# Conv input held in SBUF, three kinds of load on another queue, transposes for a broadcast, and one-operand steps on ScalarE, in a two-layer hybrid decoder trunk

## The chip, the cores and the metric

The kernel runs on one core of one Trainium2 chip. The metric is the device time of one execution in microseconds (us). Engines are named as the profile names them: PE is TensorE (PEld its weight loads), DVE is VectorE, ACT is ScalarE, POOL is GpSimd, SP is SyncE, which here only issues DMAs. POOL issues DMAs too, through a queue of its own.

## The reference, cut to what matters

Two layers over 1024 tokens of width 1024, all in float32. Each layer is

```
u = rmsnorm(h) @ W_in                       # split among three head groups
A = sparse attention: an indexer of 16 heads scores every causal key, the 256
    best keys per query are kept, softmax attention runs over them (8 heads)
B = conformer conv: y = a * sigmoid(g); causal depthwise conv of width 31;
    y = silu(layernorm(y + conv_b)); y @ conv_pw            # 256 channels
C = trailing means over 2/4/8/16 tokens minus the token, a small matmul, a scale
h += rmsnorm(concat(A, B, C) @ W_out)
h += rmsnorm(relu(rmsnorm(h) @ W_up)^2 @ W_down)
h += sigmoid(h @ W_gate) * (p @ W_ple)
```

## The kernel before, in words

Channels lie on the 128 lanes, tokens along the row; a row is half the sequence, 512 tokens ("hf" 0 or 1). Every large product is a *unit*: one 128-wide block of output channels, 24 matmuls of 128x512 (three per block of 128 input channels, since operands are split into a high and a low part; `dense`, L239). Weights come on SP's queue into two `wraw` buffers (`prepare`, L196), ACT writes the high part (L204), POOL the low part (L205). A unit's output lies in one of three PSUM buffers `pd`; five more, `bank`, serve everything else.

The order is written out in `PHASES`: a *win* phase (input projection, 21 units) and an *m* phase (output projection, MLP, gate: about 80 units) for each layer and half. Beside the units run the conv, the pooling and the attention of the halves whose projection is done, as generators in the list `bg`. `run` (L1074) gives them a share: each unit adds its cost times the phase's entry of `RATES` to a budget, each step of a generator spends some. This fixes the order of the program; a planner then fills each engine's queue by simulated times, preferring what is earlier in the program. At run time each engine, and each DMA queue, works its list strictly in order.

Buffers are rings (`Ring`, L98): `get` takes the one that was given back longest ago, and the planner adds a wait when its last user is on another engine. `dtmp` (11 rows of 512), `ctmp` (5), `row` (5 of 1088 columns) matter here.

- **Conv** (`conv_pool`, L455). In the win phase the gated input y is made in a `dtmp` (L385, L391) and stored to HBM (`cpS`, L392). `window` (L468) reads 30 + 512 columns of both channel blocks back into a `row`. Then 62 taps on DVE, each a 128x512 step into a bank (L535 for tap 0, L537 for the others). The layer norm takes a mean over the 256 channels: `token_sums` (L294: matmuls against a column of ones), a division on DVE (L551), and `spread` (L300: four matmuls against an identity that copy a value per token to all lanes). The tail (L565 to L571) ends in two more matmul groups.
- **rms** (L305): token sums, one small step on DVE, a power on POOL, `spread`. It runs in every norm: `rms_sb`, `post_norm`, and the conv.
- **Selection** (`select`, L655), the 256 best keys of each query: 31 rounds of bisection on 16-bit halves of the scores. A round counts for each of the blocks how many scores lie below a trial value. In the second half (hf 1) there are four blocks, of 640, 768, 896 and 1024 keys: ACT counts the two middle ones (L683), DVE the other two (L669), and each count writes flags that nobody reads into a scratch buffer of the ring `spare`, which in hf 1 is the ring `row`; two of its buffers are held by the 16-bit halves. Ahead of and behind the rounds stand row-wide multiplications (L713, L742) and the step that makes the mask (L755).
- **Attention** (`attend`, L815) uses `row` for the probabilities in hf 1: two for the step at hand, two for the one before.
- **Loads** on POOL's queue: keys (`kd`, L613), values (`vst`, L836), queries (`qst`, L608), and the eight inputs of the output projection (`slot<-mixS`, L923).

Of the kernel before, what the change touches and what calls it, by code (L numbers as in the profile page):

```python
# [8 lines left out]
F32 = mybir.dt.float32  # L9
# [6 lines left out]
AF = mybir.ActivationFunctionType  # L16
OP = mybir.AluOpType
# [16 lines left out]

RATES = (1.171, 1.114, 0.558, 0.766, 0.722, 0.567, 0.741, 0.946)

# [50 lines left out]
def tile_trunk(ctx: ExitStack, tc: tile.TileContext, xT, pT, pos, vecs, invf, cinv,  # L87
# [28 lines left out]
    vS = dram.tile([DEPTH, 2, P, 8, P], F32, name="vS")  # L116
    cpS = dram.tile([DEPTH, 512, S], F32, name="cpS")
    eS = dram.tile([DEPTH, NK, P, S], F32, name="eS")
# [6 lines left out]
    wlo = Ring("wlo", 4, [P, 4, P], F32R)  # L125
    dtmp = Ring("dtmp", 11, [P, HALF])
    ctmp = Ring("ctmp", 5, [P, HALF])
    cmat = Ring("cmat", 6, [P, HALF], F32R)
    rows = Ring("row", 5, [P, 1088])
    qst = Ring("qst", 2, [P, 4, P], F32R)  # L130
# [20 lines left out]
    sy.dma_start(cv, cinv)  # L151
    jp = const.tile([P, P], F32, name="jp")
    gp.iota(jp, pattern=[[1, P]], base=0, channel_multiplier=-1, allow_small_or_imprecise_dtypes=True)
    ident = const.tile([P, P], F32, name="ident")
    ve.tensor_scalar(ident, jp, 0.0, None, op0=OP.is_equal)
    ones = const.tile([P, 1], F32, name="ones")
    ve.memset(ones, 1.0)
    mhalf = const.tile([P, 4], F32, name="mhalf")
    ve.memset(mhalf, -0.5)
# [3 lines left out]
    ve.memset(cbias, 0.0)  # L163
    ve.tensor_scalar(cbias[:, P:], jp, 0.0, -BIG, op0=OP.is_gt, op1=OP.mult)
    wiT = const.tile([P, DEPTH, 8, 16], F32, name="wiT")
    rbs = Ring("rb", 1, [P, HALF])


    fr = const.tile([P, 2], F32, name="fr")
    halfpi = const.tile([P, 1], F32, name="halfpi")  # L170
    ve.memset(halfpi, math.pi / 2)
    sc.activation(halfpi, halfpi, AF.Copy)
# [127 lines left out]
    def spread(ps, t4):  # L300

        for j in range(4):
            te.matmul(ps[:, j * P:(j + 1) * P], t4[:, j:j + 1].to_broadcast([P, P]), ident, start=True, stop=True)

# [20 lines left out]
    def win_phase(l, hf, xs, sq):  # L325
# [12 lines left out]

        def evac(ps, lanes=slice(0, P), half=False):
            x = dtmp.get()  # L340
            if half:
                ve.scalar_tensor_tensor(x[lanes], ps[lanes], 0.5, rb[lanes], op0=OP.mult, op1=OP.mult)
            else:
                ve.tensor_tensor(x[lanes], ps[lanes], rb[lanes], op=OP.mult)
            return x
# [31 lines left out]
        held = None  # L377
        conv = {}
        for name in win_order(l, hf):
# [4 lines left out]
            if kind == "A":  # L384
                conv[name[1]] = evac(ps, half=True)  # L385
            elif kind == "G":
                c = int(name[1])
                g = scaled(ps)
                sc.activation(g, g, AF.Tanh, scale=0.5)
                y = conv[name[1]]  # L390
                ve.scalar_tensor_tensor(y, g, 1.0, y, op0=OP.add, op1=OP.mult)  # L391
                sy.dma_start(cpS[l, c * P:(c + 1) * P, ts], y)  # L392
                dtmp.put(y)
            elif kind == "P":
                c = int(name[1])
                x = evac(ps)
                sy.dma_start(cpS[l, 256 + c * P:256 + (c + 1) * P, ts], x)
                dtmp.put(x)
                if c == 1:
                    bg.append(((l, hf), conv_pool(l, hf)))  # L400
            elif name in ("M0", "I0"):
# [52 lines left out]

    def conv_pool(l, hf):  # L455
        t0 = hf * HALF
# [10 lines left out]

        def window(r0, n):  # L468

            t = rows.get()  # L470
            x = t[:, :2 * (n + HALF)].rearrange("p (c t) -> p c t", c=2)
            src = cpS[l, r0:r0 + 256].rearrange("(c p) t -> p c t", p=P)
            if hf == 0:
                gp.memset(x[:, :, :n], 0.0)
                sy.dma_start(x[:, :, n:], src[:, :, ts])
            else:
                sy.dma_start(x, src[:, :, t0 - n:t0 + HALF])
            return t, x
# [14 lines left out]
        wt, cw = small_weights(0, 2)  # L493
        pt_, pus = window(256, 15)
        for c in range(2):
# [29 lines left out]

        yt, yc = window(0, TAPS - 1)
        at = rows.get()
        acc = at[:, :1024].rearrange("p (c t) -> p c t", c=2)
        for c in range(2):
            pa = banks.get()  # L530
            for k in range(TAPS):
                w = vl[:, V_DW + c * TAPS + k:V_DW + c * TAPS + k + 1]
                src = yc[:, c, k:k + HALF]
                if k == 0:
                    ve.tensor_scalar(pa, src, w, vl[:, V_CONV_B + c:V_CONV_B + c + 1], op0=OP.mult, op1=OP.add)  # L535
                else:
# [4 lines left out]
        rows.put(yt)  # L541
        while (l, hf) == (0, 0) and ("index", l, hf) not in state:
# [4 lines left out]
        gp.tensor_tensor(both, acc[:, 0], acc[:, 1], op=OP.add)  # L547
        token_sums(ps, [both])
        ctmp.put(both)
        mu = tiny("mu")  # L550
        ve.tensor_scalar(mu, ps[:, :4], 1.0 / 256, None, op0=OP.mult)  # L551
        spread(ps, mu)
        sq = [ctmp.get(), ctmp.get()]
# [9 lines left out]
        for c in range(2):  # L563
            a = acc[:, c]
            ve.scalar_tensor_tensor(a, a, vl[:, V_LN_G + c:V_LN_G + c + 1], ps, op0=OP.mult, op1=OP.mult)  # L565
            th = ctmp.get()
            sc.activation(th, a, AF.Tanh, scale=0.5, bias=hb[:, l, c:c + 1])
            ve.tensor_scalar(a, a, vl[:, V_LN_B + c:V_LN_B + c + 1], 0.5, op0=OP.add, op1=OP.mult)
# [18 lines left out]
    def attention(l, hf):  # L587
# [23 lines left out]
        def load_k(h, k0, n):  # L611
            for dup in range(2):
                gp.dma_start(kd[dup * 64:(dup + 1) * 64, :, k0:k0 + n],  # L613
                             kS[l, :, :, :n].rearrange("k (d h) t -> h d k t", h=3)[h])
# [16 lines left out]
        def index():  # L631

            load_k(2, 0, Ws[-1])
            for j, b in enumerate(sel):
                W = Ws[j]
                for h in range(16):
                    if h % 4 == 0:
                        q = load_q(qiS, b, h, 16)
                    w = wiT[:, l, b, h:h + 1]
                    for n0, n1, ps in scores(q[:, h % 4], W, 0):  # L640
                        r, at = ps[:, :n1 - n0], idx[j][:, n0:n1]
                        sc.activation(r, r, AF.Relu)  # L642
                        if h == 0:
                            ve.tensor_scalar(at, r, w, None, op0=OP.mult)
                        else:
                            ve.scalar_tensor_tensor(at, r, w, at, op0=OP.mult, op1=OP.add)  # L646
                        banks.put(ps)
                    if h % 4 == 3:
                        qst.put(q)
                    yield W * 1.32 / 1024  # L650
                gp.affine_select(idx[j][:, W - P:], idx[j][:, W - P:], pattern=[[-1, P]], compare_op=OP.is_ge,
                                 fill=LOW, base=0, channel_multiplier=1)
            state["index", l, hf] = True

        def select():  # L655
# [56 lines left out]
            for j in range(nb):  # L712
                ve.tensor_scalar(idx[j], idx[j], sg[:, j:j + 1], None, op0=OP.mult)  # L713
                w0 = Ws[j - 1] if j % 2 else 0
                top.append(packed[j // 2].bitcast(I16)[:, w0:w0 + Ws[j]])
                ve.tensor_copy(top[j], idx[j].bitcast(I16)[:, 1::2])
# [24 lines left out]
            for j in range(nb):  # L741
                ve.tensor_scalar(idx[j], idx[j], sg[:, j:j + 1], None, op0=OP.mult)  # L742
            count(idx, thr, OP.is_gt, need)
# [3 lines left out]
            for j in range(nb):  # L747
# [6 lines left out]
                ve.scalar_tensor_tensor(idx[j], idx[j], thr[:, j:j + 1], e, op0=OP.is_gt, op1=OP.add)  # L754
                ve.tensor_scalar(idx[j], idx[j], -1.0, BIG, op0=OP.add, op1=OP.mult)  # L755
                spare.put(et, ct)
# [58 lines left out]
        def attend(some, at, ring):  # L815
# [3 lines left out]
            for step in [(kv, b, g) for kv in range(2) for b in some for g in (0, 2)] + [None]:  # L819
# [10 lines left out]
                if before:  # L830
                    (bkv, bb, bg), bpr = before
                    v0 = 4 * bkv if hf == 0 else 0
                    if bg == 0:
                        po = banks.get()
                        if bb == some[0]:
                            gp.dma_start(vst[:, v0:v0 + n // P], vS[l, bkv, :, :n // P])  # L836
                    yield from weighted(po, bb, (bg, bg + 1), v0, bpr, ring)
# [83 lines left out]
    def load(xs, ks, ts):  # L921
        for k in ks:
            gp.dma_start(xs[k], mixS[:, k * P:(k + 1) * P, ts].rearrange("k p t -> p k t"))  # L923

# [239 lines left out]
```

## Time and profile before

| | |
|---|---|
| time, median of 3 runs | 2843.78 us (2837.95 to 2844.03) |
| the profiled execution's own time | 2843.85 us |
| its span | 2842.1 us |
| PE busy / share of the chain that ended last | 2720.5 us / 72% |
| DVE busy / share of the chain | 1747.6 us / 16% |
| ACT busy / share of the chain | 1548.1 us / 3% |
| POOL busy / share of the chain | 1418.0 us / 1% |
| DMA, share of the chain | 5% |
| mean granted TensorE clock | 0.985 of 2.4 GHz |

The span runs from the first to the last instruction; the time of the execution holds 1.75 us more around it. Busy time of PE is the union of overlapping matmuls: one 128x512 matmul is on record for 0.39 us, but in a steady stretch a new one starts every 0.23 us. The chain goes back from the last instruction to whatever released each step, so its shares say what the end waited for, and the busy shares only what ran.

### The profile page before, as it was taken

The page shows a single profiled execution, that of the slowest core. Times are in us where ns is not written, and L with a number is a line of the kernel's source. Part 1 is how long each engine was busy: PE and PEld are TensorE (multiplying, and loading weights), DVE is VectorE, ACT ScalarE, POOL GpSimd, SP SyncE. Part 2 cuts the span into 40 slices and gives each one's busy share as a digit, 9 for nine tenths or more (in the row PEclk, how much of TensorE's full clock was granted, in tenths as well). Part 3 has the DMA queues.
Part 4 walks back from the last instruction along what each step waited for, and adds up shares of the span by engine and source line. Part 5 has one row for each costly group of instructions (what it writes and reads, how often), then busy time and mean ns, then how long its engine had stood idle before and what let it go on. Part 6 is the DMA issues. An engine that isn't in the chain of part 4 may idle for free.

```text
span 2842.1 us, 37724 instructions
## 1 busy us (share of the span) xinstructions
PE 2720.5 (96%) x12648; PEld 2242.8 (79%) x12648; DVE 1747.6 (61%) x3473; ACT 1548.1 (54%) x2932; POOL 1418.0 (50%) x1161
## 2 busy tenths in 40 slices
PE   7899989999999999899999989999999999999998
PEld 6677777887888878778788777888878878788886
DVE  7969679788447775965822467587985561511123
ACT  5347667775567535766334423677757654533343
POOL 4655425444334665544544755444443356544446
PEclk9999999999999999999999999999999999999999
DMA  5676554422343576533333547534223354423233
GB/s 189 198 192 218 153 134 148 112 85 90 93 115 106 159 238 187 162 116 102 114 104 104 184 152 238 152 116 108 97 79 98 104 164 138 155 97 99 98 97 122
DMA packets 195666, 384.90 MB, mean 135 GB/s; under 512 B 17424, under 2 KB 76944, under 8 KB 195472
## 3 DMA queue, kind: packets, MB, share of 16 engines
q1 hardware_dynamic: 138192, 330.58, 35.7%
q0 software_dynamic: 57280, 51.91, 8.7%
q8 instruction: 100, 1.64, 0.3%
q14 instruction: 94, 0.77, 0.1%
HBM read 307.97 MB, written 74.45 MB: 135 GB/s over the span
## 4 chain that ended last, share of the span: by engine, by line
PE 72%; DVE 16%; DMA 5%; ACT 3%; issue 3%; POOL 1%; SPq 0%; POOLq 0%; DVEq 0%; ACTq 0%
PE pd L243 20%; PE pd L249 20%; PE pd L248 20%; PE bank L601 5%; DVE bank L537 2%; PE bank L789 2%; DVE dtmp L875 1%; DVE row L669 1%; DVE slot L261 1%; DMA row<-cpS 1%; PE bank L798 1%; PE bank L797 1%; DVE cmat L261 1%; PE pd L298 1%; DVE dtmp L261 1%
## 5 line engine op out<-in xcount | busy, mean ns | idle before, releaser
L205 POOL TENSOR_TENSOR wlo<-wraw,whi 128x512 fp32r<-128x512 f32 x824 | 1094.7, 1334 | 1180.6 <-ACT whi L204 1115.4
L243 PE MATMUL pd<-slot,whi 128*128 128x512 f32 x3296 | 1306.8, 397 | 50.7 <-DVE slot L261 14.5
L248 PE MATMUL pd<-slot,whi 128*128 128x512 f32 x3168 | 1246.0, 393 | 4.6 <-DVE slot L261 2.7
L249 PE MATMUL pd<-slot,wlo 128*128 128x512 f32 x3168 | 1241.9, 393 | 4.1 <-POOL wlo L205 4.0
L204 ACT ACTIVATE whi<-wraw 128x512 fp32r<-128x512 f32 x824 | 511.1, 627 | 731.3 <-PE pd L248 499.0
L243 PEld LDWEIGHTS pd<-slot,whi 128*128 128x128 f32 x3296 | 625.6, 190 | 188.4 <-DVE slot L261 16.6
L249 PEld LDWEIGHTS pd<-slot,wlo 128*128 128x128 f32 x3168 | 600.0, 189 | 130.9 <-POOL wlo L205 7.5
L248 PEld LDWEIGHTS pd<-slot,whi 128*128 128x128 f32 x3168 | 601.1, 190 | 125.8 <-DVE slot L266 3.9
L601 PE MATMUL bank<-kd,qst 128*128 128x512 f32 (+3 forms) x1024 | 261.5, 360 | 10.6 <-DVE mxc L767 3.7
L646 DVE SCALAR_TENSOR_TENSOR idx<-bank,wiT,idx 128x512 f32<-128x512 f32 (+3 forms) x300 | 189.3, 652 | 94.7 <-ACT bank L642 90.7
L601 PEld LDWEIGHTS bank<-kd,qst 128*128 128x128 f32 x1024 | 181.7, 192 | 46.6 <-DVE idx L646 6.8
L642 ACT ACTIVATE bank<-bank 128x512 f32<-128x512 f32 (+2 forms) x320 | 153.8, 506 | 90.0 <-PE bank L601 85.2
L981 DVE SCALAR_TENSOR_TENSOR pd<-pd,rb 128x512 f32<-128x512 f32 x112 | 77.7, 694 | 183.2 <-PE pd L249 183.2
L995 DVE TENSOR_TENSOR yT<-yT,pd 128x512 f32<-128x512 f32 x96 | 65.5, 684 | 197.8 <-PE pd L249 197.5
L537 DVE SCALAR_TENSOR_TENSOR bank<-row,vec,bank 128x512 f32<-128x512 f32 x232 | 162.1, 746 | 0.5
L669 DVE TENSOR_SCALAR_CACHE_REDUCE row<-row,cc 128x640 f32<-128x640 uint16 (+1 forms) x124 | 133.5, 1077 | 14.5 <-ACT row L683 12.6
L683 ACT ACTIVATE row<-row,cc 128x768 f32<-128x768 uint16 (+1 forms) x124 | 121.5, 983 | 18.0 <-DVE cc L689 15.3
L767 DVE CUSTOM_DVE_ANT_0 row<-bank,idx 128x512 f32<-128x512 f32 (+3 forms) x160 | 91.4, 591 | 64.0 <-PE bank L601 60.6
L261 DVE TENSOR_TENSOR cmat<-bank,cmat 128x512 fp32r<-128x512 f32 (+1 forms) x160 | 97.9, 631 | 49.4 <-ACT cmat L260 43.8
L261 DVE TENSOR_TENSOR slot<-pd,slot 128x512 fp32r<-128x512 f32 x112 | 76.6, 685 | 51.3 <-ACT slot L260 51.1
L982 ACT ACTIVATE pd<-pd 128x512 f32<-128x512 f32 x112 | 65.2, 582 | 72.8 <-DVE pd L981 72.7
L775 ACT ACTIVATE row<-row,nmc 128x384 f32<-128x384 f32 (+5 forms) x96 | 84.2, 878 | 27.8 <-DVE nmc L771 21.0
(216 smaller groups left out, 2828.7 us busy)
## 6 DMA issues: line engine op xcount, KB each, us to landing
wraw<-wup SPq DMA_DIRECT2D x128, 512.0 KB, 3.3
wraw<-wdown SPq DMA_DIRECT2D x128, 512.0 KB, 3.3
wraw<-win SPq DMA_DIRECT2D x84, 512.0 KB, 4.2
qiS<-dtmp SPq DMA_DIRECT2D x64, 256.0 KB, 2.5
slot<-mixS POOLq DMA_DIRECT2D x32, 512.0 KB, 7.0
wraw<-wgate SPq DMA_DIRECT2D x32, 512.0 KB, 3.6
qst<-qiS POOLq DMA_DIRECT2D x48, 256.0 KB, 3.7
hS<-yT SPq DMA_DIRECT2D x48, 256.0 KB, 3.6
```

Source lines behind the costliest of these rows:

```text
L204: sc.activation(hi, r, AF.Copy)
L205: gp.tensor_tensor(lo, r, hi.bitcast(F32), op=OP.subtract)
L243: te.matmul(ps, wh, xh, start=i == 0, stop=False)
L248: te.matmul(ps, wh, xl, start=False, stop=False)
L249: te.matmul(ps, wl, xh, start=False, stop=i == n - 1)
L261: ve.tensor_tensor(lo, src, hi.bitcast(F32), op=OP.subtract)
L537: ve.scalar_tensor_tensor(acc[:, c] if k == TAPS - 1 else pa, src, w, pa, op0=OP.mult, op1=OP.add)
L601: te.matmul(ps[:, :n1 - n0], q, kd[:, k, k0 + n0:k0 + n1], start=k == 0, stop=k == 1)
L642: sc.activation(r, r, AF.Relu)
L646: ve.scalar_tensor_tensor(at, r, w, at, op0=OP.mult, op1=OP.add)
L669: ve.tensor_scalar(flags[:, :Ws[j]], of[j], t, None, op0=op, op1=OP.add, accum_out=dst[:, j:j + 1])
L683: sc.activation(flags[:, :Ws[j]], of[j], AF.Sign, scale=-1.0, bias=c[:, j:j + 1], accum_out=cnt[:, j:j + 1])
```

## The change

- `spread` uses TensorE's transpose in place of a matmul.
- The conv's input is written straight into one of two new buffers `win` (two channel blocks of 30 + 512 columns). The 30 columns in front are zeros in the first half; in the second they are a copy (ACT) of the last 30 of the first half, kept in `halo`. Only the pooling's input still goes through HBM (`plS`). Tap 0 moves to ACT.
- The conv's mean is one matmul of 128x512 against a 128x128 matrix of 1/256, which gives the mean on all lanes; token sums, division and spread go.
- On ACT in place of DVE: tap 0 (L535), the step L568, the index's first head (L644), and in the selection L713, L742 and L755.
- On SP's queue in place of POOL's: `kd`, `vst` and `slot<-mixS`. The queries stay.
- `dtmp` has 9 buffers (was 11), `row` 4 (was 5). Three of the eight `RATES` change.

```
-RATES = (1.171, 1.114, 0.558, 0.766, 0.722, 0.567, 0.741, 0.946)
+RATES = (1.205, 1.114, 0.558, 0.766, 0.751, 0.567, 0.731, 0.946)
-    dtmp = Ring("dtmp", 11, [P, HALF])
+    dtmp = Ring("dtmp", 9, [P, HALF])
-    rows = Ring("row", 5, [P, 1088])
+    rows = Ring("row", 4, [P, 1088])
+    wins = Ring("win", 2, [P, 2, TAPS - 1 + HALF])
+    halo = const.tile([P, 2, TAPS - 1], F32, name="halo")
...
-            te.matmul(ps[:, j * P:(j + 1) * P], t4[:, j:j + 1].to_broadcast([P, P]), ident, start=True, stop=True)
+            te.transpose(ps[:, j * P:(j + 1) * P], t4[:, j:j + 1].to_broadcast([P, P]), ident)
...
-                conv[name[1]] = evac(ps, half=True)
+                c = int(name[1])
+                if c == 0:
+                    yc = wins.get()
+                    if hf == 0:
+                        gp.memset(yc[:, :, :TAPS - 1], 0.0)
+                    else:
+                        sc.activation(yc[:, :, :TAPS - 1], halo, AF.Copy)
+                ve.scalar_tensor_tensor(yc[:, c, TAPS - 1:], ps, 0.5, rb, op0=OP.mult, op1=OP.mult)
...
-                y = conv[name[1]]
+                y = yc[:, c, TAPS - 1:]
                 ve.scalar_tensor_tensor(y, g, 1.0, y, op0=OP.add, op1=OP.mult)
-                sy.dma_start(cpS[l, c * P:(c + 1) * P, ts], y)
-                dtmp.put(y)
+                if c == 1 and hf == 0:
+                    sc.activation(halo, yc[:, :, HALF:], AF.Copy)
...
-        yt, yc = window(0, TAPS - 1)
...
-                    ve.tensor_scalar(pa, src, w, vl[:, V_CONV_B + c:V_CONV_B + c + 1], op0=OP.mult, op1=OP.add)
+                    sc.activation(pa, src, AF.Identity, scale=w, bias=vl[:, V_CONV_B + c:V_CONV_B + c + 1])
...
-        token_sums(ps, [both])
+        te.matmul(ps, mean256, both, start=True, stop=True)
         ctmp.put(both)
-        mu = tiny("mu")
-        ve.tensor_scalar(mu, ps[:, :4], 1.0 / 256, None, op0=OP.mult)
-        spread(ps, mu)
...
-                gp.dma_start(kd[dup * 64:(dup + 1) * 64, :, k0:k0 + n],
+                sy.dma_start(kd[dup * 64:(dup + 1) * 64, :, k0:k0 + n].bitcast(F32),
...
-                ve.tensor_scalar(idx[j], idx[j], sg[:, j:j + 1], None, op0=OP.mult)
+                sc.activation(idx[j], idx[j], AF.Copy, scale=sg[:, j:j + 1])
...
-                ve.tensor_scalar(idx[j], idx[j], -1.0, BIG, op0=OP.add, op1=OP.mult)
+                sc.activation(idx[j], idx[j], AF.Identity, scale=BIG, bias=nbig)
...
-            gp.dma_start(xs[k], mixS[:, k * P:(k + 1) * P, ts].rearrange("k p t -> p k t"))
+            sy.dma_start(xs[k].bitcast(F32), mixS[:, k * P:(k + 1) * P, ts].rearrange("k p t -> p k t"))
```

## Rows read from the trace of the kernel before

**Rows 1.** The page: busy time of each engine with its share of the span, and the chain that ended last by engine.

```profile
PE 2720.5 (96%) x12648; PEld 2242.8 (79%) x12648; DVE 1747.6 (61%) x3473; ACT 1548.1 (54%) x2932; POOL 1418.0 (50%) x1161
...
PE 72%; DVE 16%; DMA 5%; ACT 3%; issue 3%; POOL 1%; SPq 0%; POOLq 0%; DVEq 0%; ACTq 0%
```

**Rows 2.** Busy time by stretch: start and end, length, then busy us (instructions) of PE, PEld, DVE, ACT, POOL, the granted clock, the DMA share, GB/s. In order: units alone (a late MLP), the conv stages of (layer 0, half 0), (0, 1), (1, 0) and (1, 1), the rounds of the hf 1 selection of layer 0 and its tail, the rounds and the tail of layer 1, and the end of the win phase ahead of the m phase of (0, 1).

```profile
2450.00:2730.00 280.00, 280.00 (x1241) 232.02 (x1240) 54.67 (x78) 104.51 (x175) 135.45 (x105) 1.00 0.30 99
...
50.00:150.00 100.00, 82.15 (x331) 65.01 (x331) 87.93 (x121) 36.65 (x63) 56.00 (x45) 0.90 0.62 197
...
955.00:1055.00 100.00, 96.45 (x464) 79.36 (x463) 83.36 (x117) 33.79 (x60) 66.33 (x57) 1.00 0.67 199
1335.00:1400.00 65.00, 62.56 (x285) 50.83 (x284) 60.94 (x91) 21.24 (x37) 32.93 (x29) 1.00 0.42 128
1660.00:1750.00 90.00, 80.94 (x347) 65.31 (x345) 78.44 (x103) 27.02 (x47) 53.84 (x45) 0.96 0.62 193
...
606.00:659.00 53.00, 53.00 (x235) 43.92 (x234) 44.92 (x124) 42.51 (x84) 23.50 (x19) 1.00 0.30 98
660.00:695.00 35.00, 28.62 (x115) 22.51 (x113) 34.97 (x46) 11.65 (x22) 16.47 (x10) 0.90 0.22 69
2017.00:2075.00 58.00, 58.00 (x257) 48.04 (x257) 52.60 (x134) 45.13 (x88) 27.53 (x21) 1.00 0.29 97
2075.00:2112.00 37.00, 30.30 (x127) 24.34 (x126) 36.90 (x48) 12.52 (x23) 16.32 (x11) 0.95 0.22 74
...
1050.00:1088.00 38.00, 38.00 (x186) 32.19 (x185) 19.22 (x30) 18.06 (x36) 19.07 (x17) 1.00 0.71 218
```

**Rows 3.** Groups of PE instructions by line: the transposes of the attention, then token sums (L298) and spreads (L303) of the norms and of the conv; busy us and mean ns, then the idle time ahead of them.

```profile
L789 PE MATMUL bank<-ident,row 128*128 128x128 f32 x528 | 77.0, 276 | 1.4 <-DVE ctmp L807 1.4
...
L303 PE MATMUL pd<-ident,rrd 128*128 128x128 f32 x64 | 9.9, 297 | 5.0 <-POOL rrd L311 5.0
...
L303 PE MATMUL pd<-ident,rrn 128*128 128x128 f32 x64 | 8.7, 274 | 0.0
...
L298 PE MATMUL bank<-ones,ctmp 128*128 128x1 f32 x64 | 7.6, 239 | 0.0
L303 PE MATMUL bank<-ident,muc 128*128 128x128 f32 x32 | 4.2, 274 | 0.0
L303 PE MATMUL bank<-ident,rrc 128*128 128x128 f32 x32 | 4.2, 274 | 0.0
```

**Rows 4.** The conv's way through HBM: who waited for the DMAs of `cpS` (us, times), and the group of tap 0 (busy us, mean ns, idle ahead of it).

```profile
  DVE bank L535: 19.7, 4
  POOL row L499: 15.4, 4
...
L535 DVE TENSOR_SCALAR bank<-row,vec 128x512 f32<-128x512 f32 x8 | 6.3, 809 | 19.7 <-DMA row<-cpS 19.7
```

**Rows 5.** One-operand steps. First the DVE time of L713, L742 and L755 over the whole span, one line each in this order; then the spread of L755 (min/median/max ns); then ACT multiplying a row by a factor per lane (L777), widest and narrowest of six widths.

```profile
0.00:2842.10 2842.10, 8.88 (x12) 0.98 0.45 135
...
0.00:2842.10 2842.10, 9.20 (x12) 0.98 0.45 135
...
0.00:2842.10 2842.10, 12.12 (x12) 0.98 0.45 135
...
L755 DVE TENSOR_SCALAR idx<-idx x12: 517/828/1634, 304.1 to 2115.1; 128x384 f32<-128x384 f32 x2, 128x512 f32<-128x512 f32 x2, 128x640 f32<-128x640 f32 x2, 128x768 f32<-128x768 f32 x2
...
L777 ACT ACTIVATE row<-row,ric 128x1024 f32<-128x1024 f32 x16 | 18.2, 1144 | 0.7 <-DVE ric L776 0.7
...
L777 ACT ACTIVATE row<-row,ric 128x384 f32<-128x384 f32 x16 | 9.4, 607 | 0.7 <-DVE ric L776 0.7
```

**Rows 6.** One round of the selection of layer 1, hf 1, in order of time (start us, us, engine): first DVE, then ACT.

```profile
2029.15 0.88 DVE L669 TENSOR_SCALAR_CACHE_REDUCE row<-row,cc 128x640 f32<-128x640 uint16 x1
...
2030.27 1.28 DVE L669 TENSOR_SCALAR_CACHE_REDUCE row<-row,cc 128x1024 f32<-128x1024 uint16 x1 [0.16 <-ACT row L683]
...
2032.05 0.88 DVE L669 TENSOR_SCALAR_CACHE_REDUCE row<-row,cc 128x640 f32<-128x640 uint16 x1
...
2029.21 0.94 ACT L683 ACTIVATE row<-row,cc 128x768 f32<-128x768 uint16 x1 [0.20 <-DVE cc L689]
2030.05 0.19 ACT L683 ACTIVATION_READ_ACCUMULATOR row<-row,cc 128x1 f32 x1
...
2031.08 0.19 ACT L683 ACTIVATION_READ_ACCUMULATOR row<-row,cc 128x1 f32 x1
```

**Rows 7.** Loads: issue time on POOL (min/median/max ns) of the eight inputs; median landing times of POOL's and SP's loads of 512 KB; the longest waits of SP's queue and PE's wait for the inputs (us in total, times, longest).

```profile
L923 POOL DMA_DIRECT2D slot<-mixS x32: 696/733/805, 170.2 to 2334.2; - x32
...
wraw<-win SPq DMA_DIRECT2D x84, 512.0 KB, 4.2
slot<-mixS POOLq DMA_DIRECT2D x32, 512.0 KB, 7.0
...
SPq L199 <- POOL wlo L205: 1677.3, 377, 20.5
...
PE pd L243 <- DMA slot<-mixS: 5.0, 2, 2.8
```

**Rows 8.** The norm behind the MLP, last phase: POOL's five additions in a row, and the landing of the rows they add.

```profile
2789.05 8.07 POOL L876 TENSOR_TENSOR yT<-dtmp,dtmp 128x512 f32<-128x512 f32 x5 [1.89 <-DVE dtmp L875]
...
dtmp<-hS SPq DMA_DIRECT2D x48, 256.0 KB, 3.2
```

More of the change, by code (lines that the diff above doesn't have):

```diff
@@ L116, in tile_trunk @@
     vS = dram.tile([DEPTH, 2, P, 8, P], F32, name="vS")
-    cpS = dram.tile([DEPTH, 512, S], F32, name="cpS")
+    plS = dram.tile([DEPTH, 256, S], F32, name="plS")
     eS = dram.tile([DEPTH, NK, P, S], F32, name="eS")
@@ L151, in tile_trunk @@
     sy.dma_start(cv, cinv)
-    jp = const.tile([P, P], F32, name="jp")
+    lent = dtmp.get()
+    jp = lent[:, :P]
     gp.iota(jp, pattern=[[1, P]], base=0, channel_multiplier=-1, allow_small_or_imprecise_dtypes=True)
@@ L157, in tile_trunk @@
     ve.memset(ones, 1.0)
+    mean256 = const.tile([P, P], F32, name="mean256")
+    ve.memset(mean256, 1.0 / 256)
     mhalf = const.tile([P, 4], F32, name="mhalf")
@@ L164, in tile_trunk @@
     ve.tensor_scalar(cbias[:, P:], jp, 0.0, -BIG, op0=OP.is_gt, op1=OP.mult)
+    dtmp.put(lent)
     wiT = const.tile([P, DEPTH, 8, 16], F32, name="wiT")
@@ L170, in tile_trunk @@
     halfpi = const.tile([P, 1], F32, name="halfpi")
+    nbig = const.tile([P, 1], F32, name="nbig")
+    ve.memset(nbig, -BIG)
     ve.memset(halfpi, math.pi / 2)
@@ L337, in table, with evac @@
             return out
-        def evac(ps, lanes=slice(0, P), half=False):
+        def evac(ps, lanes=slice(0, P)):
             x = dtmp.get()
[L341 to L344, printed above, removed]
+            ve.tensor_tensor(x[lanes], ps[lanes], rb[lanes], op=OP.mult)
             return x
@@ L377, in win_phase @@
         held = None
-        conv = {}
         for name in win_order(l, hf):
@@ L396, in win_phase @@
                 x = evac(ps)
-                sy.dma_start(cpS[l, 256 + c * P:256 + (c + 1) * P, ts], x)
+                sy.dma_start(plS[l, c * P:(c + 1) * P, ts], x)
                 dtmp.put(x)
                 if c == 1:
-                    bg.append(((l, hf), conv_pool(l, hf)))
+                    bg.append(((l, hf), conv_pool(l, hf, yc)))
             elif name in ("M0", "I0"):
@@ L451, in win_phase, with conv_pool @@
         rbs.put(rb)
-    def conv_pool(l, hf):
+    def conv_pool(l, hf, yc):
         t0 = hf * HALF
@@ L466, in small_weights, with window @@
             return (hi, lo), [(hi[:, j * P:(j + 1) * P], lo[:, j * P:(j + 1) * P]) for j in range(n)]
-        def window(r0, n):
+        def window(n):
             t = rows.get()
             x = t[:, :2 * (n + HALF)].rearrange("p (c t) -> p c t", c=2)
-            src = cpS[l, r0:r0 + 256].rearrange("(c p) t -> p c t", p=P)
+            src = plS[l].rearrange("(c p) t -> p c t", p=P)
             if hf == 0:
@@ L493, in conv_pool @@
         wt, cw = small_weights(0, 2)
-        pt_, pus = window(256, 15)
+        pt_, pus = window(15)
         for c in range(2):
@@ L540, in conv_pool @@
             banks.put(pa)
-        rows.put(yt)
+        wins.put(yc)
         while (l, hf) == (0, 0) and ("index", l, hf) not in state:
@@ L567, in conv_pool @@
             sc.activation(th, a, AF.Tanh, scale=0.5, bias=hb[:, l, c:c + 1])
-            ve.tensor_scalar(a, a, vl[:, V_LN_B + c:V_LN_B + c + 1], 0.5, op0=OP.add, op1=OP.mult)
+            sc.activation(a, a, AF.Identity, scale=0.5, bias=hb[:, l, c:c + 1])
             ve.scalar_tensor_tensor(th, th, 1.0, a, op0=OP.add, op1=OP.mult)
@@ L643, in index @@
                         if h == 0:
-                            ve.tensor_scalar(at, r, w, None, op0=OP.mult)
+                            sc.activation(at, r, AF.Copy, scale=w)
                         else:
@@ L741, in select @@
             for j in range(nb):
-                ve.tensor_scalar(idx[j], idx[j], sg[:, j:j + 1], None, op0=OP.mult)
+                sc.activation(idx[j], idx[j], AF.Copy, scale=sg[:, j:j + 1])
             count(idx, thr, OP.is_gt, need)
@@ L835, in attend @@
                         if bb == some[0]:
-                            gp.dma_start(vst[:, v0:v0 + n // P], vS[l, bkv, :, :n // P])
+                            sy.dma_start(vst[:, v0:v0 + n // P].bitcast(F32), vS[l, bkv, :, :n // P])
                     yield from weighted(po, bb, (bg, bg + 1), v0, bpr, ring)
```

## The prediction

> **What bounds the kernel now.** I read the page first: PE is busy 96% of the span and carries 72% of the chain that ended last; DVE carries 16%, though it is busy only 61% [rows 1]. So mostly PE is the limit, and in some stretches DVE is. The view by stretch says which. A late MLP shows PE alone: 1241 matmuls in 280 us, 0.2256 us each, at full clock [rows 2]; a unit of 24 costs 5.4 us, and nothing but fewer or shorter PE instructions helps there. The four conv stages look different. In 50 to 150 DVE is busy 87.9 of 100 us, PE idles 17.85 and the granted clock falls to 0.90; the idle time of PE in the other three is 3.55, 2.44 and 9.06 us, 32.9 in all [rows 2]. Here a late DVE holds PE up. In the rounds of the selection PE has no idle time at all, but in the two tails behind them DVE is full (34.97 of 35, 36.90 of 37 us) and PE idles 6.38 and 6.70 us [rows 2]. The gains must come from these three places: PE's own work, conv stages, tails.
>
> **1. Spread by transposes, mean by one matmul.** A spread is recorded as 8 matmuls, two per block; the attention's transposes of the same 128x128 blocks have one record each, 77.0/528 = 0.146 us [rows 3]. The 160 records of the norms' spreads take 9.9 + 8.7 + 4.2 = 22.8 us; 80 transposes at 0.146 take 11.7: 11.1 us less. The mean loses its spread (4.2) and half of the conv's token sums (3.8), and gets one full-precision matmul of 512 columns in each of four stages; by columns that equals a spread, so 4.2 in all: 3.8 less. Sum 14.9 us. All of it is PE work, and a spread is also a link of its norm's chain, so nearly all counts; I take -14, with ends -16 and -7 (half of it idles instead).
>
> The terms of "TensorE: Matmul & The Clock Gate" in the Trainium skill call transpose mode four times faster for float32. By that the norms' spreads would fall to 5.7 us and this term to about -21. The attention's transposes here stand at half the records of the matmul form, not a quarter, so the sum goes by the row.
>
> **2. The conv input in SBUF.** DVE stood 19.7 us before tap 0, waiting for the four reads of `cpS`; tap 0 itself costs DVE 6.3 us [rows 4]. Both go, 26 us of DVE over four stages. Next late is the gated input itself, then ACT's tap 0, one 128x512 step on an engine that is busy 21 to 37 us of each such stage [rows 2]. What queues behind DVE's wait for it is tap 1 and, if ACT is late, the evacuation of PE's units. PE can win at most its 32.9 us of idle time, and only where DVE is full: about 7 us in the first stage, 4 in the last, none in the middle two, where PE idles under 4%. I take -11; ends -30 and 0. L568 on ACT frees DVE for eight short steps behind the taps: nothing. The pooling still comes through HBM, and its wait on POOL (15.4) stays [rows 4].
>
> **3. One-operand steps on ACT.** L713, L742 and L755 hold DVE 8.88 + 9.20 + 12.12 = 30.2 us; 36 ACT steps between 0.607 and 1.144, mean 0.876, take 31.5 [rows 5]. The selection's own chain thus stays as long, and DVE is freed of 30 us, of which only L755 stands in a tail: four steps, some 4 us in each hf 1 tail, of PE's 13.1 us of idle time there. The softmax then waits for ACT instead. I take -3; ends -10 and +5. The index's first head (L644) lies where neither engine is full: nothing.
>
> The rules of "ScalarE: Activation LUTs" in the Trainium skill speak against this: a plain multiplication or addition belongs on VectorE. A median step of L755 on DVE does take 0.828 us, but single ones reach 1.634 [rows 5]. By the medians the move loses a little time per step, by the measured sums nearly none, and the sum goes by these.
>
> **4. One `row` less.** This edit costs, and the diff does not show it. In hf 1 the selection's scratch comes from `row`: five less two packed ones is three, and now two. A round takes four: ACT, ACT, DVE, DVE. With three, only DVE's second count waits, for ACT's first; the row of the 1024 count says so: 0.16 us, released by L683. With two, DVE's first count waits for ACT's first (ends 2030.24) and its second for ACT's second (ends 2031.27). In the round shown DVE's second count starts at 2030.27; it would start at 2031.27: 1.0 us more on a round of 2.90 [rows 6]. That is 31 us in each of two selections, 62 in all. PE is full through the rounds [rows 2], and the evacuations of the units fit into the new gaps, so the time is only lost if the attention behind ends late: for half 1 of layer 0, ahead of the m phase at 1088, DVE has 38.0 - 19.2 = 18.8 us to spare [rows 2]. I take +6; ends 0 and +62. In the attention four buffers are just what two steps hold; PE is full there: nothing.
>
> **5. Loads on SP's queue.** Issuing one input takes POOL 0.733 us, and 512 KB land in 7.0 us; SP's weight loads of that size land in 4.2 [rows 7]. PE waited 5.0 us for the inputs, and POOL, which makes the weights' low parts, loses 76 issues. Against it: SP stands 1677 of 2842 us, 4.4 each time, waiting for a weight buffer [rows 7]; a load planned behind that waits too, and a load that waits for its data holds the next weight load. Two weight buffers cover 2 x 5.4 us of PE, more than a landing. I take -4; ends -9 and +18 (four m phases, each one such wait late).
>
> **6. Nine `dtmp` and the rest.** The conv no longer holds any. In the norm behind the MLP four rows of the embedding and two scratch rows leave three for the residual instead of five. POOL adds one row each 8.07/5 = 1.6 us; three buffers give 4.8 us for a landing of 3.2 [rows 8]. Covered, +1; if not, one landing in each of four norms, +13. The new `RATES` only move where steps stand in the program; no row prices that: 0, between -5 and +5 by PE's idle time in a tail.
>
> **Sum.** -14 - 11 - 3 + 6 - 4 + 1 + 0 = -25 against the profiled execution's own 2843.85, which stands within 0.1 us of the median: 2819 us.
>
> **Rivals.**
> - *The rounds arrive late* (slower). If the 62 us of part 4 reach the end in place of the 6, the time is 2819 - 6 + 62 = 2875. It decides from the point where more than 31 of the 62 come through, since the other terms give -31. For it: the rounds' DVE counts stand on the chain's DVE share, and the m phase needs that attention. Against: PE is full for the whole of the rounds, so that dense work is ready, and 18.8 us of slack lie ahead of the first deadline.
> - *SP's queue pushes back* (no change). Moved loads queue behind weight waits at all four starts: +18 for -4, 2841. For it: SP waits 59% of the span. Against: stores already go through that queue, and PE's waits for DMAs are small.
> - *Only PE's own work counts.* DVE's relief is eaten by what follows on DVE in the conv stages: terms 2 and 3 are nothing: 2833. For it: DVE stays full of taps. Against: the first conv stage has 17.85 us of idle PE.
> - *The conv stages recover in full*, -30 for -11, clock included: 2800.
>
> **Chances.** A measurement of this kernel tells about 0.2% (5.7 us) from no change. Forecast 0.48 (own range 2805 to 2835), late rounds 0.14, SP's queue 0.12, PE's work only 0.14, full recovery 0.12. Faster: 0.48 + 0.12 + 0.12 from the third = 0.72, less 0.02 for a forecast that ends at its upper edge: 0.70. Same: 0.08 from SP's queue and the 0.04 left over: 0.12. Slower: 0.14 and 0.04: 0.18. The range 2796 to 2854 takes in three of the four rivals and leaves out late rounds from about two thirds on.
>
> **What would show it.** Spreads with 4 records and half the time; no wait ahead of tap 1 over 1 us; less idle PE in the first and last conv stages and a clock back towards 1.00 there; rounds of 3.9 us with DVE's first count released by L683; inputs landing in under 5 us. It is wrong if PE's idle time grows ahead of the m phases (waits for `slot` from SP, or an attention that ends late), or if waits of L204 for weights grow.

## The result, and the profile after

| | before | after |
|---|---|---|
| time, median | 2841.91 us (2837.95 to 2844.03, 4 runs) | 2804.11 us (2803.53 to 2807.1, 4 runs) |
| ratio | | 0.9871, interval 0.9854 to 0.9888 |
| span of the profiled execution | 2842.1 us | 2802.1 us |

The kernel after is 1.29% faster (1.12% to 1.46%). One part in a thousand of the ratio is 2.84 us; the ratio says 36.7 us, the medians 37.8. Of all executions below, one of u_slot took 5160.8 us at a lower granted clock (0.889); it is in that run's median, but not in its ratio. In the code after, the lines of before are shifted by 9 or so; each number below is given with what it does.

The page of the kernel after: busy time of the engines, and the chain that ended last.

```profile
PE 2701.1 (96%) x12512; PEld 2224.5 (79%) x12512; DVE 1698.4 (61%) x3399; ACT 1599.7 (57%) x3008; POOL 1372.7 (49%) x1085
...
PE 78%; DVE 10%; DMA 5%; issue 2%; ACT 2%; POOL 1%; SPq 0%; POOLq 0%; ACTq 0%; DVEq 0%
```

Against [rows 1] PE does 19.4 us less, and outside its busy time it idles 101.0 us where it idled 121.6. DVE's share of the chain falls from 16% to 10%.

PE groups of the kernel after (busy us, mean ns): the spreads of the norms (L312), the conv's mean (L560) and its token sums (L307).

```profile
L312 PE MATMUL pd<-ident,rrd 128*128 128x128 f32 x32 | 6.0, 292 | 3.0 <-POOL rrd L320 3.0
...
L312 PE MATMUL pd<-ident,rrn 128*128 128x128 f32 x32 | 4.8, 272 | 0.0
...
L560 PE MATMUL bank<-ctmp,mean 128*128 128x512 f32 x8 | 4.1, 590 | 0.0
...
L307 PE MATMUL bank<-ones,ctmp 128*128 128x1 f32 x32 | 3.8, 237 | 0.0
...
L312 PE MATMUL bank<-ident,rrc 128*128 128x128 f32 x16 | 2.4, 276 | 1.5 <-POOL rrc L320 1.5
```

Each record lasts as long as in [rows 3], but there are half as many: 13.2 us for 22.8. With the mean's 4.1 and the halved token sums PE's own work is 13.5 us less.

By stretch, after (columns as in [rows 2]): the first conv stage and the last, the tails behind the two selections, a late MLP.

```profile
50.00:150.00 100.00, 84.33 (x346) 66.73 (x344) 81.80 (x117) 40.07 (x70) 59.18 (x47) 0.93 0.65 202
...
1635.00:1725.00 90.00, 81.57 (x354) 65.53 (x353) 67.72 (x88) 33.77 (x60) 53.20 (x42) 0.96 0.65 196
675.00:710.00 35.00, 32.10 (x140) 25.35 (x139) 34.64 (x51) 12.95 (x22) 17.00 (x10) 1.00 0.22 75
2061.00:2098.00 37.00, 32.52 (x131) 25.91 (x130) 36.14 (x54) 12.73 (x22) 19.04 (x10) 0.91 0.22 72
...
2412.00:2692.00 280.00, 280.00 (x1238) 231.61 (x1238) 55.77 (x79) 105.05 (x176) 134.58 (x105) 1.00 0.29 98
```

In the conv stages DVE has room now (81.8 for 87.9, 67.7 for 78.4 us), yet PE idles 15.67 and 8.43 us there, nearly as before (17.85 and 9.06). In the tails it idles 2.90 and 4.48 (before 6.38 and 6.70). The late MLP is the same.

DVE's waits in the kernel after (us in all, times, longest): the counts of the selection (L678), the conv's taps (L549).

```profile
DVE row L678 <- ACT row L692: 56.6, 57, 1.9
...
DVE bank L549 <- ACT bank L547: 6.0, 4, 3.2
```

The 19.7 us ahead of tap 0 [rows 4] have become 6.0 ahead of tap 1. A wait that took 12.6 us before now stands above them: 57 times a count on DVE waits for one on ACT. One round of it, in order of time (start us, us), DVE first, then ACT:

```profile
606.54 0.88 DVE L678 TENSOR_SCALAR_CACHE_REDUCE row<-row,cc 128x640 f32<-128x640 uint16 x1 [0.96 <-ACT row L692]
...
607.57 1.28 DVE L678 TENSOR_SCALAR_CACHE_REDUCE row<-row,cc 128x1024 f32<-128x1024 uint16 x1
...
610.57 0.88 DVE L678 TENSOR_SCALAR_CACHE_REDUCE row<-row,cc 128x640 f32<-128x640 uint16 x1 [1.13 <-ACT row L692]
...
606.32 0.19 ACT L692 ACTIVATION_READ_ACCUMULATOR row<-row,cc 128x1 f32 x1
...
607.35 0.18 ACT L692 ACTIVATION_READ_ACCUMULATOR row<-row,cc 128x1 f32 x1
```

DVE's first count starts when ACT's first has ended (606.51), its second when ACT's second has (607.53); the round lasts 4.03 us for the 2.90 of [rows 6]. Over the 31 rounds of half 1 the trace shows 117.1 us in layer 0 and 115.3 in layer 1 before (from the first comparison step L688 to the last), 145.2 and 147.8 after: 28.1 and 32.5 us longer.

The moved loads in the kernel after: issue time on SP (min/median/max ns), the longest wait of SP's queue, PE's wait for the inputs.

```profile
L932 SPq DMA_DIRECT2D slot<-mixS x32: 370/402/783, 170.2 to 2300.8; - x32
...
SPq L208 <- POOL wlo L214: 1648.1, 374, 14.7
...
PE pd L252 <- DMA slot<-mixS: 2.3, 1, 2.3
```

### The profile page after: what moved, and what is told of

It reads as the page before. It is cut to its first block, busy times and chain, and to the rows that moved or that the text cites. A ratio compares the mean times of both kernels' runs of the same rounds, so it can differ in the third digit from the quotient of the medians.

```text
span 2802.1 us, 37352 instructions
## 1 busy us (share of the span) xinstructions
PE 2701.1 (96%) x12512; PEld 2224.5 (79%) x12512; DVE 1698.4 (61%) x3399; ACT 1599.7 (57%) x3008; POOL 1372.7 (49%) x1085
## 4 chain that ended last, share of the span: by engine, by line
PE 78%; DVE 10%; DMA 5%; issue 2%; ACT 2%; POOL 1%; SPq 0%; POOLq 0%; ACTq 0%; DVEq 0%
PE pd L252 22%; PE pd L257 22%; PE pd L258 22%; PE bank L610 6%; PE bank L798 2%; DVE bank L549 2%; PE bank L807 1%; PE bank L806 1%; DMA wraw<-win 1%; DVE row L761 1%; DVE dtmp L884 1%; PE pd L255 1%; PE pd L307 1%; POOL wlo L214 1%; DVE dtmp L270 1%
## 5 line engine op out<-in xcount | busy, mean ns | idle before, releaser
L678 DVE TENSOR_SCALAR_CACHE_REDUCE row<-row,cc 128x640 f32<-128x640 uint16 (+1 forms) x124 | 133.5, 1078 | 63.4 <-ACT row L692 56.6
L549 DVE SCALAR_TENSOR_TENSOR bank<-win,vec,bank 128x512 f32<-128x512 f32 x232 | 165.5, 746 | 7.7 <-ACT bank L547 6.0
L269 ACT ACTIVATE cmat<-bank 128x512 fp32r<-128x512 f32 (+1 forms) x160 | 83.7, 546 | 26.4 <-PE bank L798 23.1
```

The source lines that it names most:

```text
L678: ve.tensor_scalar(flags[:, :Ws[j]], of[j], t, None, op0=op, op1=OP.add, accum_out=dst[:, j:j + 1])
```

## The experiments

The first eight undo or do one part alone; the last four change only the order. Each batch has its own runs of the kernel before, so ratios are compared: after is 0.9871, and the intervals reach about 0.0015 to either side, so that two results less than about 6 us apart are not told from each other. An "us above after" below is the difference of the two ratios.

**u_spread**: after, without part 1.

```
-            te.transpose(ps[:, j * P:(j + 1) * P], t4[:, j:j + 1].to_broadcast([P, P]), ident)
+            te.matmul(ps[:, j * P:(j + 1) * P], t4[:, j:j + 1].to_broadcast([P, P]), ident, start=True, stop=True)
...
-        te.matmul(ps, mean256, both, start=True, stop=True)
+        token_sums(ps, [both])
+        mu = tiny("mu")
+        ve.tensor_scalar(mu, ps[:, :4], 1.0 / 256, None, op0=OP.mult)
+        spread(ps, mu)
```

> The changed kernel with part 1 undone: spreads as matmuls again, the conv's mean by token sums, division and spread. Theory (PE's own work counts nearly in full, term -14): some 14 us slower than the changed kernel's 2804, so 2812 to 2822; the spreads again have 8 records of 1.05 us. Rival (spreads lie in places where PE would idle anyway, and the gain came from elsewhere): 2804 to 2809.

Measured 2820.09 us (2818.27 to 2822.76), ratio 0.9923 (0.991 to 0.9936): 0.0052 or 14.8 us above after. PE's groups are those of before to 0.2 us:

```profile
L312 PE MATMUL pd<-ident,rrd 128*128 128x128 f32 x64 | 9.9, 295 | 3.2 <-POOL rrd L320 3.2
...
L312 PE MATMUL bank<-ident,muc 128*128 128x128 f32 x32 | 4.2, 274 | 0.0
```

The 14.8 us, some 6 either way, agree with the 13.5 us of PE's own work: it counts in full, as far as this run can tell.

**u_conv**: after, with the conv's input through HBM into a `row` again, tap 0 still on ACT.

```
-                    yc = wins.get()
...
+                sy.dma_start(cyS[l, c * P:(c + 1) * P, ts], y)
...
+        yt, yc = window(TAPS - 1, cyS)
```

> The changed kernel with the conv's input through HBM again, read into one of the four row buffers; tap 0 stays on ACT, dtmp stays at 9. Theory A (the gain beyond the forecast came from here, because the conv no longer waits for a row and for its round trip, and so starts earlier in layer 0 half 1 and layer 1 half 0): 2822 to 2835. Theory B (the term is the -11 that was forecast): 2812 to 2818. Rival (planner's order, not the conv): 2800 to 2809.

Measured 2807.11 us (2805.38 to 2813.97), ratio 0.9878 (0.9864 to 0.9893): 2 us above after, not told from it. What the reads of HBM now delay, by the waits of ACT and of DVE:

```profile
DVE bank L543 <- ACT bank L541: 8.1, 2, 6.1
ACT bank L541 <- DMA row<-cyS: 2.8, 1, 2.8
```

DVE waits 8.1 us for tap 0 here and 6.0 in the kernel after: without the HBM trip the taps start little earlier. The time is in the range of the rival (2800 to 2809), outside those of both theories.

**u_act**: after, with all moved one-operand steps back on DVE.

```
-                sc.activation(idx[j], idx[j], AF.Copy, scale=sg[:, j:j + 1])
+                ve.tensor_scalar(idx[j], idx[j], sg[:, j:j + 1], None, op0=OP.mult)
...
-                sc.activation(idx[j], idx[j], AF.Identity, scale=BIG, bias=nbig)
+                ve.tensor_scalar(idx[j], idx[j], -1.0, BIG, op0=OP.add, op1=OP.mult)
```

> The changed kernel with all one-operand steps back on DVE: tap 0, L568, the index's first head, the three of the selection. Theory (term -3, mostly in the two tails): 2805 to 2810, tails as full of DVE as before the change. Rival (freeing DVE of 50 us of work is what gave the extra gain): 2814 or more. Other rival (the steps are better on DVE): below 2800.

Measured 2808.18 us (2807.91 to 2808.55), ratio 0.9878 (0.9865 to 0.989): 2 us above after. The two tails by stretch:

```profile
692.00:727.00 35.00, 28.16 (x124) 23.08 (x123) 34.82 (x37) 6.90 (x11) 20.74 (x11) 0.95 0.28 90
2075.50:2112.50 37.00, 32.28 (x133) 26.30 (x131) 36.74 (x51) 8.92 (x16) 17.98 (x11) 0.91 0.23 72
```

PE idles 6.84 and 4.72 us here, 2.90 and 4.48 in the kernel after: 4.2 us less idle time, nearly all of it in the first tail. The time is in the range of the theory, but so close to after that it proves no price.

**u_load**: after, with keys, values and inputs back on POOL's queue.

```
-                sy.dma_start(kd[dup * 64:(dup + 1) * 64, :, k0:k0 + n].bitcast(F32),
+                gp.dma_start(kd[dup * 64:(dup + 1) * 64, :, k0:k0 + n],
...
-                            sy.dma_start(vst[:, v0:v0 + n // P].bitcast(F32), vS[l, bkv, :, :n // P])
+                            gp.dma_start(vst[:, v0:v0 + n // P], vS[l, bkv, :, :n // P])
...
-            sy.dma_start(xs[k].bitcast(F32), mixS[:, k * P:(k + 1) * P, ts].rearrange("k p t -> p k t"))
+            gp.dma_start(xs[k], mixS[:, k * P:(k + 1) * P, ts].rearrange("k p t -> p k t"))
```

> The changed kernel with keys, values and the output projection's inputs back on POOL's queue. Theory (term -4): 2806 to 2811, landing of the inputs near 7 us again. Rival (SP's queue pushes back, so that the move cost time): 2796 to 2802. Other rival (freeing POOL of 76 issues is the extra gain): 2814 or more.

Measured 2841.68 us (2832.2 to 2848.52), ratio 0.9993 (0.9982 to 1.0005): 34.7 us above after, and no faster than before. The theory that freeing POOL is an extra gain had said 2814 or more; a loss of this size was expected by none. Waits of POOL in this run, then of PE:

```profile
POOL slot L932 <- DMA mixS<-ctmp: 15.1, 4, 4.9
...
POOL kd L622 <- PE bank L610: 11.9, 4, 6.0
POOL vst L845 <- PE bank L610: 10.2, 2, 9.5
...
PE pd L252 <- ACT whi L213: 16.1, 9, 7.0
...
PE pd L258 <- POOL wlo L214: 7.6, 5, 2.6
```

POOL stands before loads whose data or buffer is not ready, and the weights' low parts behind them wait. One way in which that may reach PE can be followed at the last start (POOL, SP and ACT in turn):

```profile
2322.36 2.90 POOL L932 DMA_DIRECT2D slot<-mixS  x4 [4.94 <-DMA mixS<-ctmp]
2325.25 1.30 POOL L214 TENSOR_TENSOR wlo<-wraw,whi 128x512 fp32r<-128x512 f32 x1
...
2326.57 0.33 SPq L208 DMA_DIRECT2D wraw<-wgate  x1
...
2334.40 1.15 ACT L213 ACTIVATE whi<-wraw 128x512 fp32r<-128x512 f32 x2 [4.62 <-DMA wraw<-wgate]
```

POOL waits 4.94 us for the last store, issues four loads in 2.90, and only then makes a low part; that frees a weight buffer, SP loads it, ACT gets it late, and PE's longest wait there is 3.5 us. The next runs ask whether this is the cause. A second thing stands beside it: the span is 33.5 us longer, but PE's idle time grew by only 22.6 of them (123.6 us for 101.0). The other 10.9 are busy time, 2712.0 us for 2701.1, for the same 12512 matmuls:

```profile
PE 2712.0 (96%) x12512; PEld 2229.7 (79%) x12512; DVE 1718.6 (61%) x3399; ACT 1598.9 (56%) x3008; POOL 1415.0 (50%) x1161
```

**u_slot** and **u_kd**: after, with only the inputs, or only keys and values, back on POOL (the third line of the diff above, or the first two).

> The kernel after with only the inputs of the output projection back on POOL's queue (32 loads of 512 KB that wait for the stores of the heads' outputs). Theory A (these loads stand in front of the weights' low parts at the start of each m phase and are the costly ones): 2825 or more, most of the 37.6 us. Theory B (keys and values are, see the next run): 2808 or less. Theory C (both share it): about 2815 to 2825.

> The kernel after with only keys and values back on POOL's queue (they wait until PE has read the keys or values before them). Theory A: the inputs of the output projection are the costly ones: 2808 or less here. Theory B: keys and values hold POOL in the middle of dense work, 2825 or more. Theory C: both share it, 2815 to 2825.

Measured 2819.01 us (2815.19 to 2820.75 without the execution of 5160.8), ratio 0.9908 (0.9892 to 0.9923), for u_slot and 2830.05 us (2825.53 to 2831.36), ratio 0.9947 (0.9934 to 0.9959), for u_kd: 10.5 and 21.6 us above after, 32.1 together for u_load's 34.7. Keys and values are the larger part (their theory, 2825 or more, holds), and the inputs have a share (2815 to 2825). PE's waits in u_kd from 2300 to 2332 us, the same start as above, and SP's queue in it:

```profile
PE pd L252 <- ACT whi L213: 5.7, 3, 3.7
...
2314.97 1.91 SPq L932 DMA_DIRECT2D slot<-mixS  x4
```

Here the inputs come through SP, and PE loses the same time (u_load: 5.9, its longest wait 3.5). So POOL's wait for the last store is not needed for this loss. What both runs share is an attention of the last half that ends late against the dense work: its last store is issued 50 us after the gate's first weight load in u_load and u_kd, 44 us in u_slot and in the kernel after, and in these two PE has no wait over 0.9 us there. That is no cause either: u_act issues this store 63 us after, and PE has no wait over 0.9 us there; flags (below), with all three kinds of load on SP's queue, issues it 47 us after, and PE waits 6.4 us for the weights' high parts, against u_load's 5.9. PE's waits in flags, over the whole span, then from 2245 to 2318 us:

```profile
PE pd L252 <- ACT whi L213: 15.1, 6, 6.5
...
PE pd L258 <- POOL wlo L214: 6.2, 6, 2.7
...
PE pd L252 <- ACT whi L213: 6.4, 2, 5.3
```

Over the span PE waits for the weights' parts nearly as long in flags (15.1 and 6.2 us) as in u_load (16.1 and 7.6), and flags is 2 us above after. So PE's waits for weights do not account for u_load's 34.7 us. Taking each block from its first weight load to that of the next, u_kd loses 11.0 us up to the end of the input projections of layer 0, and 10.9 in the gate ahead of the last output projection; the rest comes and goes.

**b_load**: before, with part 5 alone (the diff of u_load, the other way).

> The kernel before with part 5 alone: keys, values and the eight inputs of the output projection are loaded through SP's queue. Undoing this part in the kernel after cost 37.6 us. Theory A (POOL's own order): a load that waits for its data on POOL holds up the weights' low parts behind it whatever else the kernel does, so the move gives most of that here too: 2815 or less. Theory B (it only counts together with the other parts, which make POOL's or PE's order tighter): here it gives the 4 us of the prediction, 2834 to 2842. Theory C (SP's queue pushes back as long as the conv's rows go through it as well): 2845 or more.

Measured 2835.54 us (2829.42 to 2841.87), ratio 0.9969 (0.9958 to 0.9979): 8.8 us faster than before. In the kernel before POOL stood as long for the same loads (values 12.0 and 8.2, keys 9.4, inputs 8.4 and 7.9 us) as in u_load, so the length of those waits alone doesn't set what they cost. The result is the one expected if the move counts fully only together with the other parts; it refutes the theory that POOL's order costs the same whatever else the kernel does (2815 or less).

**flags**: after, with part 4's wait taken away by other scratch buffers.

```
+                    flags = spare.get()
...
-                        flags = spare.get()
...
-                        spare.put(flags)
-                    count(of, c, OP.is_lt, cnt, [j for j in range(nb) if j not in acts])
+                    other = spare.free.pop(0)
+                    for j in range(nb):
+                        if j not in acts:
+                            ve.tensor_scalar(other[:, :Ws[j]], of[j], c[:, j:j + 1], None, op0=OP.is_lt, op1=OP.add,
+                                             accum_out=cnt[:, j:j + 1])
+                    spare.free[:0] = [flags, other]
```

> The kernel after with other scratch buffers in the selection's rounds of the second half: ACT's two counts write their flags to one buffer and DVE's two to another, so that no count of one engine waits for the other; the four rows stay four. A round should fall from 4.0 to 2.9 us or less, 31 us in each of two selections. Theory of the prediction (part 4, of the 62 us 6 reach the end): 2798. Rival (late rounds, most of it reaches the end): 2780 or less. Rival (all of it is hidden by PE's dense work): 2801 to 2807.

DVE's counts in one round:

```profile
2018.38 0.88 DVE L697 TENSOR_SCALAR_CACHE_REDUCE row<-row,cc 128x640 f32<-128x640 uint16 x1
...
2019.30 1.28 DVE L697 TENSOR_SCALAR_CACHE_REDUCE row<-row,cc 128x1024 f32<-128x1024 uint16 x1
...
2021.08 0.88 DVE L697 TENSOR_SCALAR_CACHE_REDUCE row<-row,cc 128x640 f32<-128x640 uint16 x1
```

No count waits for ACT, the round takes 2.70 us, and the 31 rounds take 114.6 and 110.7 us for 145.2 and 147.8. The time is 2809.11 us (2805.57 to 2810.94), ratio 0.9877 (0.9862 to 0.9892): not faster. Of 68 us given back to the selections nothing that can be told reaches the end.

**u_rates, u_mid, u_load_rates, b_rates**: another order and nothing else. u_rates is after with the `RATES` of before, u_mid with values half way, u_load_rates is u_load with the `RATES` of before, b_rates is before with those of after.

```
-RATES = (1.205, 1.114, 0.558, 0.766, 0.751, 0.567, 0.731, 0.946)
+RATES = (1.171, 1.114, 0.558, 0.766, 0.722, 0.567, 0.741, 0.946)
...
+RATES = (1.188, 1.114, 0.558, 0.766, 0.737, 0.567, 0.736, 0.946)
```

> The kernel after with the RATES of before: no instruction is added or taken away, only the order of the program changes. The prediction put this at 0, between -5 and +5: 2799 to 2809. Theory O (the order of the program is itself worth tens of microseconds, and the terms found by undoing one part each hold such a share, since every edit makes the planner lay out the whole program anew): 2812 or more.

> The kernel after with RATES half way between those of before and its own: again the same work in another order. Theory O: off by 5 us or more from 2804 as well, to either side, and not in between the two other sets in any orderly way. Rival (the rates act smoothly, the order hardly counts): between 2804 and the result of the run before, within 3 us of their mean.

> The kernel after with all moved loads back on POOL's queue, as in the run that lost 37.6 us, and also the RATES of before. Theory P (POOL's queue, blocked in order by loads that wait, costs the 37 us whatever the order): 2835 to 2848. Theory O (a large part of the 37 us is the order that the planner made around these loads): 2830 or less, since another order can win back what that one lost.

> The kernel before with the RATES of after: the same work in another order. Theory O: 5 us or more away from 2843, to either side. Rival (the order is worth little): 2838 to 2848.

| run | time, us | ratio (interval) | against the same kernel with its own rates |
|---|---|---|---|
| u_rates | 2810.16 | 0.9882 (0.9863 to 0.9901) | +3 us |
| u_mid | 2804.59 | 0.9864 (0.9844 to 0.9883) | -2 us |
| u_load_rates | 2830.29 | 0.9946 (0.9926 to 0.9966) | -13 us |
| b_rates | 2854.9 | 1.0038 (1.0026 to 1.0049) | +11 us |

The order alone moves a time by up to 13 us. For the kernel after it is within the interval, and a value half way gives no surprise; but for u_load and before it is clear of the interval and as much as most terms of the prediction. So each "undo" carries such a share, and a result of 2 us (u_conv, u_act, flags) names no price.

## Why the prediction came out as it did

The forecast was 2819 us, 25 below; measured are 37 below, in its range, 1 us beyond the forecast's own. Three runs, in order, make a path of steps with a result each. All parts but part 5, with the old rates (u_load_rates, 0.9946): -15.3 us. Part 5 on top (u_rates, 0.9882): -18.2. The new rates (after, 0.9871): -3.1. Each step is uncertain by some 6 to 8 us.

That the sum came near is in part luck. Parts 2, 3, 4 and 6 were forecast at -7 together, and beside part 1's 14.8 us the first step leaves them about -1; part 5, forecast at -4, gave 18. For parts 2 and 3 the rival "only PE's own work counts" was nearer than the forecast.

Of the signs named in advance, the halved spreads came, and so did the longer rounds with DVE's first count behind ACT's. The wait ahead of tap 1 was up to 3.2 us and not under 1. The clock went from 0.90 to 0.93 in the first conv stage and stayed at 0.96 in the last. Where the landing of the inputs on SP's queue is on record it is 5.5 us (b_load) and 6.7 us (u_kd), not under 5.

- **Part 1, -14: right.** Undone it costs 14.8 us, and PE's groups account for 13.5. PE's share of the chain, 72% before and 78% after, fits that it counts in full. By "TensorE: Matmul & The Clock Gate" in the Trainium skill (its terms) a float32 transpose is four times faster; this trace has a factor of two in records, 4 for 8 of equal length, as the attention's rows had promised, and of 1.7 in busy time (22.8 to 13.2 us, forecast 11.7).
- **Part 2, -11: oversized.** Undone it costs 2 us, not told from nothing. The failing step is "Here a late DVE holds PE up", with its price of 7 us in the first stage and 4 in the last. DVE's 19.7 us did shrink to 6.0 and the first conv stage has DVE at 81.8%, yet PE still idles 15.67 us of 17.85. PE's two longest waits there before, then 50 to 160 us before and after, and PE's wait in that stretch that is new after:

```profile
PE bank L243 <- ACT cmat L260: 8.0, 2, 5.3
PE pd L243 <- DVE dtmp L261: 6.6, 1, 6.6
...
50.00:160.00 110.00, 92.15 (x377) 73.47 (x377) 95.68 (x133) 42.94 (x76) 62.71 (x52) 0.91 0.63 197
...
50.00:160.00 110.00, 92.05 (x378) 73.67 (x377) 88.68 (x129) 45.54 (x82) 61.90 (x50) 0.91 0.66 201
...
152.28 3.52 PE L610 MATMUL bank<-kd,qst 128*128 128x384 f32 x10 [6.32 <-DMA qst<-qiS]
```

  Before, PE's waits name DVE for 9.5 us and ACT, which splits the pooled input, for 8.0; the pooling still comes through HBM. After, PE idles only 11.7 us up to 146 us, and then 6.3 us for the load of the first queries, so that from 50 to 160 us both kernels run as many matmuls (377 and 378) and idle as long (17.85 and 17.95 us): what DVE gave back was lost again at the next link. In the last stage PE's waits name DVE for 8.1 of 8.4 us still, though DVE is busy 67.7 of 90: one late step is enough (5.0 us, L371), and a fuller or emptier engine says little.
- **Part 3, -3: in line, not proven.** 4.2 us of idle time go from the tails, and the total moves by 2 us.
- **Part 4, +6: the mechanism right, no price seen.** The rounds grew by 61 us for the 62 forecast, with the wait where it was said to be. Taking it away gained nothing that can be told, so late rounds, the slower rival, are refuted. PE is busy for all of 559 to 659 us in the kernel after, so it has dense work through these rounds; that the attention behind meets no deadline was not looked at by itself.
- **Part 5, -4 with an end at -9: mis-sized.** It is -18.2 in the path (and 34.7 undone at the new rates), though alone in the kernel before it is -8.8, just the end given. The failing step priced only PE's own wait for the inputs (5.0 us) and POOL's 76 issues. The keys and values, which the prediction counted only among these issues, cost twice as much as the inputs (21.6 and 10.5 us). That POOL's order counts, in which a load that waits holds the work behind it, is the likely reason, but it is not shown: PE's waits for weights are as long in flags, and POOL's waits as long in the kernel before. The feared wait in SP's queue stayed away: PE waited 2.3 us for inputs. "DMA: Bandwidth & Descriptors" in the Trainium skill gives simple loads to Sync (its table of issuing engines), and the runs agree; its sentence that the time to initiate is "usually small relative to the DMA itself" agrees with 0.733 us of issue beside 7.0 of landing [rows 7].
- **Part 6, +1 and 0.** The new rates gained 3 us for the kernel after, within the 5 allowed and within the interval; on the kernel before they cost 11. The nine `dtmp` alone were not tried.

What stays open: why part 5 is worth 9 us in the kernel before and 18 to 35 beside the other parts, with POOL's waits of the same length. The runs show that the order carries up to 13 us of it. A rival was not tried: the loads also land later from POOL's queue, 7.0 to 7.2 us for the inputs where SP's queue has 5.5 and 6.7, and no run separates that from POOL's order.

## What to carry to other kernels

A load on an engine that also computes can cost far more than its issue time and than PE's wait for it, here 9 to 35 us by the kernel around it: try the move, and in more than one order. A wait found in the slower kernel is no cause before you have looked for it in the faster ones. Before you price a stretch by one full engine and one idle one, find the wait that names the other; the fuller engine may be a neighbour. And where a planner lays out the program anew after every edit, measure the same work in another order first: edits that gain less than that can't be judged one by one.

## What was not expected of the hardware

The same 512 KB load took POOL 0.733 us to issue [rows 7] and SP 0.402. And in u_kd, after a wait of 2.27 us in the middle of dense work, PE's matmuls started 0.43 us apart instead of 0.23 for some 3.5 us:

```profile
285.88 0.50 PE L252 MATMUL pd<-slot,whi 128*128 128x512 f32 x1 [2.27 <-ACT whi L213]
...
288.27 0.63 PE L257 MATMUL pd<-slot,whi 128*128 128x512 f32 x1
288.69 0.63 PE L258 MATMUL pd<-slot,wlo 128*128 128x512 f32 x1
...
283.20:290.00 6.80, 4.53 (x15) 3.44 (x14) 5.29 (x26) 6.30 (x19) 5.07 (x4) 0.75 0.61 203
```

The granted clock of that stretch (283.2 to 290) was 0.75, between the two levels of 1.2 and 2.4 GHz, and 1.00 in the stretches before and behind it, so that a short wait on PE cost more than its own length. Likewise the granted clock was 0.96 in u_load from 2269 to 2348 us, where the kernel after has 1.00 from 2252 to 2318: probably a part of u_load's longer busy time.
